# Attention scores with the query's two parts stacked on 128 partitions, in a two-layer hybrid encoder

## The chip, the core and the metric

The kernel runs on one core of a Trainium2 chip. The metric is device time in microseconds (us) of one execution, from the first to the last work on the core: 1370.9 us in the median of three runs before the change (1370.58 to 1371.35). A profile shows one further execution.

## What is computed

Two layers of an encoder over 512 tokens of 1024 channels, in float32. A layer normalizes x (an RMS norm with a scale and a shift made from a conditioning vector), projects it by `w_in` to 28 column blocks of 128, and hands these to three mixers: a gated depthwise convolution of width 31 over 256 channels, attention with 6 heads of 64, and a bidirectional gated recurrence (HGRN2) with 6 heads of 64. Their outputs together go through `w_out` into the residual. Then comes a gated MLP with a depthwise convolution of width 3. The attention is what matters here:

```python
scores = jnp.einsum('bnqhd,bnkhd->bhqk', qb, kb) * (Dh ** -0.5)   # Dh = 64
scores = scores - slopes[:, None, None] * dist
lse = jax.nn.logsumexp(scores, axis=-1)
p = jnp.exp(scores - lse[..., None])
...
wts = jax.nn.softmax(jnp.stack(lses, 0), axis=0)      # over three window/dilation pairs
att = jnp.einsum('gbsh,gbshd->bshd', wts, jnp.stack(outs, 0))
```

(The indices are cut.) The three windows with their mixture are one softmax over all 512 keys with a bias table a head, which is how the kernel computes it.

## The kernel before

**Layout.** Activations lie transposed, channels on the 128 partitions and the 512 tokens along the free dimension. TensorE multiplies in fp32r, so each operand of a large product is split into a high part, rounded to fp32r, and a low part, the rest: a product is three matmuls, high by high, high by low and low by high. The weights are split on the chip as they arrive (`wr` is the raw chunk, `wh` and `wl` its parts), the activations when they are made (`hx`).

**Engines.** Every TensorE matmul passes through the helper `mm` (L274), transposes through L280, and all work of VectorE (DVE) and ScalarE (ACT) through a wrapper (L181), so the profile's groups are told apart by tiles. SyncE (SP) issues all DMAs: weights, the tables for the conditioning (`wa`, `bias` from `w_ada`), and the attention's bias tables.

**Order.** The program is made of generators ("threads") that yield what they need next. A planner keeps a clock for each engine with a cost for each operation, and always lets run the thread of the best priority whose needs are met by that clock. What comes out is one fixed order of instructions on each engine. `span` tells the planner which stretch of a buffer an operand covers, and `written` when that stretch is ready. SBUF buffers come from small pools by tag (`BUFFERS`: size in KB a partition, count); what the MLP and the weight splitter keep is also taken from the pools of `MTAG`, `qk` among them.

**Mixers.** The projections run one column block after another (`REST`), 24 matmuls of 512 columns each into one of two PSUM banks `g`. `evac` takes a block out of PSUM. For the attention, a block of q or k holds a pair of heads, head 0 on partitions 0 to 63 and head 1 on 64 to 127. `evac` makes the high part with one ScalarE instruction (for k with whichever of ScalarE and VectorE the planner finds sooner) and the low part with one VectorE instruction, into one `qk` tile of two planes. There are three pairs a layer.

**Attention.** When q, k and v of a pair are out, `att` loads the two bias tables and starts eight `att_tile`, first the four query blocks of head 0 and then those of head 1, at most three under way. A tile is 128 queries by 512 keys:

```python
r = slice(64 * hd, 64 * hd + 64)
mm(sp, q[r, 0, s], k[r, 0], True, False)
mm(sp, q[r, 0, s], k[r, 1], False, False)
mm(sp, q[r, 1, s], k[r, 0], False, True)
```

These use 64 rows of the array, the upper or the lower half by the head. After it VectorE adds the bias and takes the minimum (q is negated, so the scores are too), ScalarE takes the exponential with its sum, the reciprocal and scaling follow on VectorE or ScalarE, then four transposes into PSUM and two copies into `PT`. When all eight are done, eight matmuls with v make the pair's output. The recurrence has small score matmuls of its own (64 by 32 blocks, `km`, `KK`, `QQ`).

Of the kernel before, what the change touches and what calls it, by code (L numbers as in the profile page):

```python
# [9 lines left out]
F32 = mybir.dt.float32  # L10
F32R = mybir.dt.float32r
# [8 lines left out]
T = 512  # L20
# [21 lines left out]
BUFFERS = dict(wr=(4, 3), wh=(4, 4), wl=(4, 4), hx=(4, 8), qk=(4, 2), PT=(4, 4), KK=(4, 1), QQ=(4, 1), S=(4, 1),  # L42
# [26 lines left out]
def span(ap):  # L69
    lo = hi = ap.offset  # L70
    for s, n in ap.ap[1:]:
        if s > 0:
            hi += s * (n - 1)
        else:
            lo += s * (n - 1)
    return lo, hi
# [116 lines left out]
class Kernel:  # L193
# [68 lines left out]
    def dma(self, out, in_, eng=None):  # L262
        (eng or self.nc.sync).dma_start(out=out, in_=in_)
        c = self.clk
        sb = out if in_.tensor.name in self.a_names else in_
        t = max(c.t.get("DMA", 0.0), c.t["PE"], c.written(sb) or 0.0, c.avail.get(sb.tensor.name, 0.0)) + size(sb) * sb.shape[0] * 4 / 350e3
        c.t["DMA"] = t
        if sb is out:
            lo, hi = span(out)
            c.w.setdefault(out.tensor.name, []).append((lo, hi, t + (4.5 if eng is self.nc.gpsimd else 2.4), "DMA"))  # L270
        c.last[sb.tensor.name] = t + 2.0

# [617 lines left out]
    def evac(self, l, n, ps):  # L890
# [51 lines left out]
        elif n >= Q_ATT:  # L942
            q = n < K_ATT
            p = n - Q_ATT if q else n - K_ATT
            yield (ps, "qk")
            t = self.sb([128, 2, T], "qk", F32R)
            if q:
                sc.activation(t[:, 0], ps, AF.Copy, scale=-0.125)
                yield (t[:, 0], DM)
                v.scalar_tensor_tensor(t[:, 1], ps, -0.125, t[:, 0].bitcast(F32), ALU.mult, ALU.subtract)  # L950
            else:
                self.copy(t[:, 0], ps)
                yield (t[:, 0], DM)
                v.tensor_tensor(out=t[:, 1], in0=ps, in1=t[:, 0].bitcast(F32), op=ALU.subtract)
            self.give(ps)
            cur["qa" if q else "ka", p] = t
# [243 lines left out]
    def att(self, l, p):  # L1200
# [8 lines left out]
        for hd in range(2):  # L1209
            for qt in range(4):  # L1210
                yield tuple(ths[-3:-2])
                ths.append(self.spawn(self.att_tile(q, k, bias[hd], PT[2 * hd:2 * hd + 2], hd, qt), AP, SLACK))
        yield tuple(ths) + (cur.pop(("Va", p)),)
        self.give(q, k, *bias)
# [18 lines left out]
    def att_tile(self, q, k, b, PT, hd, qt):  # L1233
        v, mm = self.v, self.mm
        r = slice(64 * hd, 64 * hd + 64)
# [3 lines left out]
        mm(sp, q[r, 0, s], k[r, 0], True, False)  # L1239
        mm(sp, q[r, 0, s], k[r, 1], False, False)  # L1240
        mm(sp, q[r, 1, s], k[r, 0], False, True)
# [195 lines left out]
```

## Time and profile before

| | |
|---|---|
| median of three runs | 1370.9 us |
| the profiled execution | 1370.76 us |
| its span, first to last instruction | 1369.0 us |
| mean granted TensorE clock | 0.991 |
| busy share of the span: PE, DVE, ACT | 98%, 78%, 45% |
| DMA | 169.19 MB, mean 124 GB/s |
| layer 0's mixers, layer 1's mixers | about 68 to 316 us, about 740 to 970 us |

The profiled execution is longer than its span by 1.8 us. In the profile PE is TensorE's matmul and PEld its weight load, a separate instruction that can run ahead of the matmuls. Matmuls overlap in their last part, so a single matmul's duration is longer than the distance to the next; costs are read from distances between starts. In a group's row stand engine, operation, output and inputs by tile name, shape, count, then busy time, the mean in ns of one, and the idle time before with what ended it. "issue" is time for which the profile shows nothing that was waited for.

### The profile page before, as it was taken

Reading aid. Unit: us, or ns where it says so; the run is one execution under the profiler, and the core shown is the slowest. Engines: PE = TensorE matmul, PEld = TensorE weight load, DVE = VectorE, ACT = ScalarE, POOL = GpSimd, SP = SyncE. Lnnn points to the kernel's source line nnn. Section 1 sums busy time; section 2 is a strip of 40 time slices with the busy share of each in tenths; the row PEclk is TensorE's granted clock in tenths of the full one; section 3 lists DMA queues with packets and bytes.
Section 4 is the critical chain, followed back from the end, with each engine's and each line's share of the span. In section 5 each row is a group of like instructions: output and inputs, shape, how many; then the busy total and the mean of one; then the engine's idle time right before and its main releaser. Section 6 shows DMA issues by size and latency. Waiting matters only on the chain.

```text
span 1369.0 us, 24502 instructions
## 1 busy us (share of the span) xinstructions
PE 1344.9 (98%) x10042; PEld 1112.4 (81%) x10042; DVE 1070.0 (78%) x1841; ACT 609.6 (45%) x1017; POOL 2.1 (0%) x16
## 2 busy tenths in 40 slices
PE   8999999999999999999999999999999999999997
PEld 7977767778988888888899777777898888888887
DVE  6799999898599999766695999888868565556666
ACT  4537556565342433333453473746535232233332
POOL 0000000000000000000000000000000000000000
PEclk8999999999999999999999999999999999999998
DMA  9534443232348788432431312011422323323221
GB/s 353 189 134 142 124 151 94 81 105 89 103 148 293 254 280 290 126 108 70 140 99 63 106 54 99 32 53 54 139 78 57 128 76 95 101 86 122 77 93 63
DMA packets 55264, 169.19 MB, mean 124 GB/s; under 512 B 6256, under 2 KB 8304, under 8 KB 55152
## 3 DMA queue, kind: packets, MB, share of 16 engines
q1 hardware_dynamic: 55152, 167.63, 37.9%
q8 instruction: 79, 1.29, 0.4%
q14 instruction: 33, 0.27, 0.1%
HBM read 165.50 MB, written 2.10 MB: 122 GB/s over the span
## 4 chain that ended last, share of the span: by engine, by line
PE 84%; DVE 12%; ACT 2%; issue 1%; DMA 0%; SPq 0%; DVEq 0%; ACTq 0%
PE m L274 53%; PE g L274 29%; DVE acc L181 2%; PE m L280 2%; DVE KK L181 2%; DVE QQ L181 1%; DVE wl L181 1%; DVE TT L181 1%; DVE wa L181 1%; DVE P L181 1%; DVE hx L181 1%; DVE x L181 1%; DVE st L181 0%; DVE sc L181 0%; DMA x<-xT 0%
## 5 line engine op out<-in xcount | busy, mean ns | idle before, releaser
L274 PE MATMUL g<-hx,wh 128*128 128x512 f32 (+1 forms) x1288 | 402.6, 390 | 0.9 <-DVE qk L181 0.8
L274 PE MATMUL m<-hx,wh 128*128 128x512 f32 (+1 forms) x1136 | 318.0, 364 | 0.0
L181 DVE TENSOR_TENSOR wl<-wr,wh 128x1024 fp32r<-128x1024 f32 (+3 forms) x215 | 220.5, 1027 | 90.4 <-ACT wh L181 79.4
L274 PEld LDWEIGHTS g<-hx,wh 128*128 128x128 f32 x1288 | 237.2, 189 | 53.2 <-issue 7.7
L181 ACT CAST wh<-wr 128x1024 fp32r<-128x1024 f32 (+3 forms) x176 | 157.1, 893 | 250.9 <-PE m L274 155.0
L274 PE MATMUL g<-hx,wl 128*128 128x512 f32 (+1 forms) x648 | 252.7, 390 | 0.0
L274 PEld LDWEIGHTS m<-hx,wh 128*128 128x128 f32 x1136 | 204.3, 189 | 34.2 <-issue 0.6
L274 PE MATMUL m<-hx,wl 128*128 128x512 f32 (+1 forms) x576 | 209.0, 363 | 0.0
L274 PEld LDWEIGHTS g<-hx,wl 128*128 128x128 f32 x648 | 122.5, 189 | 25.4 <-issue 3.8
L274 PEld LDWEIGHTS m<-hx,wl 128*128 128x128 f32 x576 | 108.7, 189 | 16.9
L181 DVE SCALAR_TENSOR_TENSOR x<-m,mod,x 128x256 f32<-128x256 f32 (+1 forms) x112 | 66.2, 592 | 43.1 <-PE m L274 42.1
L181 DVE SCALAR_TENSOR_TENSOR acc<-ap,par,acc 128x512 f32<-128x512 f32 x120 | 89.8, 748 | 2.2
L181 DVE SCALAR_TENSOR_TENSOR tmp<-m,par,tmp 128x511 f32<-128x511 f32 x120 | 89.1, 746 | 1.9
L181 ACT ACTIVATE P<-P,sm 128x512 f32<-128x512 f32 x72 | 51.5, 721 | 42.6 <-DVE sm L181 42.2
L181 ACT ACT_TABLE_LOAD x49 | 62.9, 1283 | 6.0 <-DVE sm L181 4.5
L181 DVE CAST wh<-wr 128x1024 fp32r<-128x1024 f32 (+3 forms) x41 | 24.5, 598 | 52.4 <-PE m L274 37.1
L181 ACT ACTIVATE tmp<-tmp 128x512 f32<-128x512 f32 x44 | 27.8, 632 | 73.1 <-DVE tmp L181 73.0
L181 ACT COPY km<-KK 128x512 f32<-128x512 f32 x30 | 20.5, 683 | 80.2 <-DVE KK L181 58.8
L181 ACT ACTIVATE tmp<-m,par 128x512 f32<-128x512 f32 x60 | 40.7, 686 | 34.5 <-PE m L274 32.8
L181 DVE CUSTOM_DVE_ANT_0 bias<-bias,cb,par 128x1024 f32<-128x1024 f32 x39 | 49.5, 1278 | 2.3 <-DMA bias<-w_ada 2.3
L181 DVE CUSTOM_DVE_ANT_0 wa<-wa,cb,par 128x1024 f32<-128x1024 f32 x39 | 49.9, 1278 | 0.7 <-DMA wa<-w_ada 0.7
L181 ACT ACTIVATE tmp<-x 128x256 f32<-128x256 f32 (+1 forms) x64 | 28.4, 444 | 46.4 <-DVE x L181 42.4
(319 smaller groups left out, 2158.0 us busy)
## 6 DMA issues: line engine op xcount, KB each, us to landing
wr<-w_up SPq DMA_DIRECT2D x76, 512.0 KB, 3.5
wr<-w_in SPq DMA_DIRECT2D x44, 512.0 KB, 3.5
bias<-w_ada SPq DMA_DIRECT2D x39, 512.0 KB, 4.5
wa<-w_ada SPq DMA_DIRECT2D x39, 512.0 KB, 4.0
wr<-w_down SPq DMA_DIRECT2D x32, 320.0 KB, 2.9
wr<-w_down SPq DMA_DIRECT2D x32, 256.0 KB, 2.6
wr<-w_in SPq DMA_DIRECT2D x16, 384.0 KB, 4.4
wr<-w_up SPq DMA_DIRECT2D x16, 384.0 KB, 3.3
```

The costliest lines, as they stand in the source:

```text
L181: r = f(*a, **k)
L274: self.nc.tensor.matmul(out, lhsT=lhsT, rhs=rhs, start=start, stop=stop, **kw)
L280: self.nc.tensor.transpose(out, in_, self.ident)
```

## The change

The query's high and low part of a head are put on top of each other: for head 0 the high part stays on partitions 0 to 63 and the low part is written to 64 to 127, for head 1 the other way round. The key gets a tile for each head, with the high part in plane 0 and the low part in plane 1; both are made on the head's own 64 partitions and then copied by one DMA (`shift`) to the other 64. A score tile is then two matmuls over all 128 partitions: (q high + q low) by k high, and the same by k low. The product of the two low parts, which was left out before, is now included.

So `evac` makes the parts a head at a time, on 64 partitions: two instructions where there was one, on ScalarE and on VectorE, for q and for k, and for k two DMAs on SP's queue. The `qk` pool has three buffers instead of two. `span` no longer counts the partition into the offset, so that the planner takes writes to different partition halves of a buffer as writes to the same stretch. The scratch space for dynamic DMA in SBUF is made smaller, which makes room for the buffer.

```diff
-BUFFERS = dict(wr=(4, 3), wh=(4, 4), wl=(4, 4), hx=(4, 8), qk=(4, 2), PT=(4, 4), ...
+BUFFERS = dict(wr=(4, 3), wh=(4, 4), wl=(4, 4), hx=(4, 8), qk=(4, 3), PT=(4, 4), ...
...
 def span(ap):
-    lo = hi = ap.offset
+    lo = hi = ap.offset % ap.ap[0][0]
...
+    def shift(self, out, in_):
+        self.nc.sync.dma_start(out=out.bitcast(F32), in_=in_.bitcast(F32))
+        c = self.clk
+        t = max(c.t.get("DMA", 0.0), c.t["PE"], c.written(in_) or 0.0) + size(in_) * in_.shape[0] * 4 / 350e3
+        c.t["DMA"] = t
+        lo, hi = span(out)
+        c.w.setdefault(out.tensor.name, []).append((lo, hi, t + 2.4, "DMA"))
+        c.last[out.tensor.name] = t + 2.4
...
-            yield (ps, "qk")
-            t = self.sb([128, 2, T], "qk", F32R)
+            own = [slice(0, 64), slice(64, 128)]
             if q:
-                sc.activation(t[:, 0], ps, AF.Copy, scale=-0.125)
-                yield (t[:, 0], DM)
-                v.scalar_tensor_tensor(t[:, 1], ps, -0.125, t[:, 0].bitcast(F32), ALU.mult, ALU.subtract)
+                yield (ps, "qk")
+                t = self.sb([128, 2, T], "qk", F32R)
+                for hd in range(2):
+                    sc.activation(t[own[hd], hd], ps[own[hd]], AF.Copy, scale=-0.125)
+                for hd in range(2):
+                    yield (t[:, hd], DM)
+                    v.scalar_tensor_tensor(t[own[1 - hd], hd], ps[own[hd]], -0.125, t[own[hd], hd].bitcast(F32),
+                                           ALU.mult, ALU.subtract)
             else:
-                self.copy(t[:, 0], ps)
-                yield (t[:, 0], DM)
-                v.tensor_tensor(out=t[:, 1], in0=ps, in1=t[:, 0].bitcast(F32), op=ALU.subtract)
+                yield (ps, ["qk", 2])
+                t = [self.sb([128, 2, T], "qk", F32R) for _ in range(2)]
+                for hd in range(2):
+                    self.copy(t[hd][own[hd], 0], ps[own[hd]])
+                for hd in range(2):
+                    yield (t[hd][:, 0], DM)
+                    v.tensor_tensor(out=t[hd][own[hd], 1], in0=ps[own[hd]], in1=t[hd][own[hd], 0].bitcast(F32),
+                                    op=ALU.subtract)
             self.give(ps)
+            if not q:
+                for hd in range(2):
+                    yield (t[hd],)
+                    self.shift(t[hd][own[1 - hd]], t[hd][own[hd]])
...
-        r = slice(64 * hd, 64 * hd + 64)
         s = slice(qt * 128, qt * 128 + 128)
         yield (q, k, "m")
         sp = self.pst("m")
-        mm(sp, q[r, 0, s], k[r, 0], True, False)
-        mm(sp, q[r, 0, s], k[r, 1], False, False)
-        mm(sp, q[r, 1, s], k[r, 0], False, True)
+        for i in range(2):
+            mm(sp, q[:, hd, s], k[:, i], i == 0, i == 1)
...
-    nc = bacc.Bacc("TRN2", target_bir_lowering=False, num_devices=1)
+    nc = bacc.Bacc("TRN2", target_bir_lowering=False, num_devices=1, dynamic_dma_scratch_size=1024)
```

The planner runs anew on all of this, so the order shifts throughout. Three places follow, in each the kernel before and then the changed one. A name is a buffer's tag with running numbers, so a number differs between the two kernels for the same thing; the lines are shifted by 10 (L274 is now L284).

On TensorE, the third pair of layer 0, from the last projection (V) to the first scores (`m_...<-qk,qk`):

```order
L274 MATMUL g_444_3067<-hx_18_198,wh_407_2791 128x512 x2
L274 MATMUL m_0_451_3103<-QQ_420_2874,km_442_3063 32x32 x32
L274 MATMUL g_444_3067<-hx_18_198,wl_412_2808 128x512
L274 MATMUL m_462_3159<-qk_445_3069,qk_426_2889 128x512 x3
L274 MATMUL m_463_3163<-qk_445_3069,qk_426_2889 128x512 x3
L280 MATMUL m_464_3167<-ident,tmp_453_3141 128x128 x4
```

```order
L284 MATMUL g_441_3031<-hx_18_199,wh_402_2732 128x512 x2
L284 MATMUL g_441_3031<-hx_18_199,wl_409_2761 128x512
L284 MATMUL g_460_3140<-hx_444_3046,wh_413_2798 128x512 x2
L284 MATMUL g_460_3140<-hx_444_3046,wl_416_2806 128x512
L284 MATMUL m_0_461_3144<-QQ_420_2841,km_451_3113 32x32 x32
L284 MATMUL m_463_3179<-qk_438_3021,qk_430_2909 128x512 x2
L290 MATMUL m_464_3182<-ident,tmp_453_3129 128x128 x4
```

The scores have moved behind the first three matmuls of the output projection (`g_460`), and they are two instead of three. Between the last matmul for k and the first score stand 24 full matmuls before and 27 now, with a group for the conditioning (`wa,cT`) and one more of the recurrence; for the second pair of the layer it is 27 and 32, with the same two and four transposes.

On VectorE, the first pair of layer 0, the low parts of q (`g_155`) and k (`g_163`) between steps of the recurrence (`KK`, `QQ`), the convolution (`acc`) and a weight's low part (`wl`):

```order
L181 SCALAR_TENSOR_TENSOR qk_162_1203<-g_155_1129,qk_162_1203 128x512
L181 SCALAR_TENSOR_TENSOR acc_120_866<-ap_137_935,par,acc_120_866 128x512
L181 TENSOR_TENSOR wl_172_1317<-wr_153_1125,wh_169_1278 128x1024
L181 TENSOR_TENSOR qk_170_1281<-g_163_1205,qk_170_1281 128x512
L181 TENSOR_TENSOR KK_122_869<-KK_122_869,TT_123_870 128x16x2x16
```

```order
L181 SCALAR_TENSOR_TENSOR qk_162_1204<-g_155_1130,qk_162_1204 64x512 x2
L181 TENSOR_TENSOR wl_173_1321<-wr_153_1126,wh_169_1280 128x1024
L181 TENSOR_TENSOR qk_170_1283<-g_163_1207,qk_170_1283 64x512
L181 TENSOR_TENSOR KK_123_872<-KK_123_872,TT_124_873 128x16x2x16
L181 TENSOR_TENSOR QQ_132_917<-QQ_132_917,TT_124_873 128x16x2x16
L181 COPY_PREDICATED sc_135_923<-msk,m_0_172_1288 128x256
L181 COPY S_134_922<-sc_135_923 32x8x32
L181 TENSOR_TENSOR TT_124_873<-TT_124_873 128x48
L181 TENSOR_TENSOR qk_171_1284<-g_163_1207,qk_171_1284 64x512
```

Each low part is two instructions now, and the second half of k comes after a step of the recurrence.

On SP, the DMAs of the second pair of layer 0 (`bias<-bias` are the two bias tables, `wa` and `wr` conditioning and weights):

```order
L263 DMA wr_306_2182<-w_in 128x1024
L263 DMA wa_307_2189<-w_sh 128x1024
L263 DMA bias_310_2198<-bias 128x896
L263 DMA bias_311_2199<-bias 128x896
L263 DMA wr_323_2262<-w_in 128x1024
```

```order
L263 DMA wr_308_2169<-w_in 128x1024
L263 DMA wa_309_2177<-w_sh 128x1024
L275 DMA qk_302_2112<-qk_302_2112 64x1024
L275 DMA qk_303_2113<-qk_303_2113 64x1024
L263 DMA bias_315_2240<-bias 128x896
L263 DMA bias_316_2241<-bias 128x896
L263 DMA wa_326_2278<-w_ada 128x1024
L263 DMA wr_328_2313<-w_in 128x1024
```

The two copies of k's parts stand ahead of the bias tables and of the next weights. Over the whole program VectorE has 12 more copies into `PT`, 10 fewer scalings of `P` and 4 more of the gates (`KK`, `TT`), which went from or to ScalarE.

More of the change, by code (lines that the diff above doesn't have):

```diff
@@ L39 @@
 H2 = T // 2
-BUFFERS = dict(wr=(4, 3), wh=(4, 4), wl=(4, 4), hx=(4, 8), qk=(4, 2), PT=(4, 4), KK=(4, 1), QQ=(4, 1), S=(4, 1),
+BUFFERS = dict(wr=(4, 3), wh=(4, 4), wl=(4, 4), hx=(4, 8), qk=(4, 3), PT=(4, 4), KK=(4, 1), QQ=(4, 1), S=(4, 1),
                TT=(6, 1), ao=(2, 2), vr=(2, 2), va=(2, 1), bias=(4, 2), wa=(4, 1), tmp=(2, 5), P=(2, 2), sc=(1, 1),
@@ L1211, in att @@
                 yield tuple(ths[-3:-2])
-                ths.append(self.spawn(self.att_tile(q, k, bias[hd], PT[2 * hd:2 * hd + 2], hd, qt), AP, SLACK))
+                ths.append(self.spawn(self.att_tile(q, k[hd], bias[hd], PT[2 * hd:2 * hd + 2], hd, qt), AP, SLACK))
         yield tuple(ths) + (cur.pop(("Va", p)),)
-        self.give(q, k, *bias)
+        self.give(q, *k, *bias)
         V = cur["va"]
```

## The prediction

> **What bounds the kernel now.** I read the page's engine totals and its chain first, then windows cut by stage, then the chain in order of time, and last the PE timeline around one score tile.
>
> ```profile
> PE 1344.9 (98%) x10042; PEld 1112.4 (81%) x10042; DVE 1070.0 (78%) x1841; ACT 609.6 (45%) x1017; POOL 2.1 (0%) x16
> PE 84%; DVE 12%; ACT 2%; issue 1%; DMA 0%; SPq 0%; DVEq 0%; ACTq 0%
> ```
>
> TensorE fills the span, and VectorE has the rest of the chain. The windows (span, then busy us of PE, PEld, DVE, ACT, POOL, the clock, DMA share, GB/s) say where: 68 to 316 is layer 0's mixers, 740 to 970 layer 1's, 450 to 500 a piece of an MLP.
>
> ```profile
> 68.00:316.00 248.00, 241.09 (x2639) 177.24 (x2637) 226.14 (x434) 143.40 (x256) 0.00 (x0) 0.99 0.38 118
> 740.00:970.00 230.00, 228.54 (x2544) 172.54 (x2543) 206.44 (x397) 133.63 (x239) 0.00 (x0) 1.00 0.22 71
> 100.00:120.00 20.00, 20.00 (x233) 15.65 (x233) 19.57 (x40) 11.22 (x22) 0.00 (x0) 1.00 0.56 177
> 750.00:780.00 30.00, 30.00 (x494) 23.35 (x492) 29.71 (x46) 11.30 (x19) 0.00 (x0) 1.00 0.29 92
> 180.00:250.00 70.00, 69.73 (x716) 51.47 (x716) 63.29 (x128) 43.32 (x83) 0.00 (x0) 0.98 0.40 128
> 450.00:500.00 50.00, 50.00 (x223) 41.39 (x222) 48.63 (x77) 19.07 (x28) 0.00 (x0) 1.00 0.76 245
> ```
>
> In the MLP TensorE runs without a gap, and there are no scores. In the mixers VectorE is busy 91.2% (226.1 of 248) and 89.8% (206.4 of 230), and 97.9% and 99.0% in the dense pieces: two engines share the bound there. The chain (start, length) runs over full matmuls in one place and over VectorE's steps in another:
>
> ```profile
> 380.04 10.88 PE g L274 x48
> 842.04 0.60 DVE qk L181
> 842.64 0.59 DVE KK L181
> ```
>
> So a full 512-column matmul costs 10.88/48 = 0.227 us, and a VectorE instruction of 512 columns holds the next one back 0.60.
>
> **What it removes.** Three 64-row matmuls a tile become two of 128 rows. The timeline (start, us, ...) and the weight load behind it, one tile between projections; then the first and last of the score stretches, and the one odd one; then their group:
>
> ```profile
> 137.27 0.40 PE L274 MATMUL g<-hx,wh 128*128 128x512 f32 x1
> 137.60 0.96 PE L274 MATMUL m<-qk,qk 64*128 64x512 f32 x3
> 138.49 0.50 PE L274 MATMUL g<-hx,wh 128*128 128x512 f32 x1
> 138.83 0.40 PE L274 MATMUL g<-hx,wl 128*128 128x512 f32 x1
> 138.49 0.19 PEld L274 LDWEIGHTS g<-hx,wh 128*128 128x128 f32 x1 [0.37 <-issue]
> 106.54 2.35 PE L274 MATMUL m<-qk,qk 64*128 64x512 f32 x9
> 954.56 0.96 PE L274 MATMUL m<-qk,qk 64*128 64x512 f32 x3
> 793.18 0.97 PE L274 MATMUL m<-qk,qk 64*128 64x512 f32 x6
> L274 PE MATMUL m<-qk,qk 64*128 64x512 f32 x144 | 43.2, 420 | 1.0 <-DVE qk L181 0.3 <-DVE sm L181 0.3 <-ACT tmp L181 0.2
> ```
>
> A matmul less for each of 48 tiles is 48 x 0.227 = 10.9 us. The larger part is the change of height: 137.27 to 138.83 is 1.56 us for five matmuls, and five at 0.227 are 1.14, so going to 64 rows and back costs 0.42; the weight load at 138.49 starts late, with its matmul, instead of running ahead. Nine scores in a row pay it once. The PE timeline has 38 such stretches from 106.54 to 954.56, 21 in layer 0 and 17 in layer 1. At full height they pay nothing: layer 0 saves 21 x 0.42 + 24 x 0.227 = 14.3 us, layer 1 17 x 0.42 + 5.4 = 12.6. At 793.18 two heads' tiles already run side by side (six matmuls in the time of three); that is lost, 0.7. TensorE's sum is 26.2 us, nearest possible time 1370.8 - 26.2 = 1344.6.
>
> **What it adds.**
>
> ```profile
> L181 DVE SCALAR_TENSOR_TENSOR qk<-g,qk 128x512 fp32r<-128x512 f32 x6 | 4.1, 684 | 0.0
> L181 ACT COPY S<-m 32x256 f32<-32x256 f32 x24 | 8.7, 361 | 0.2
> L181 ACT COPY PT<-m 128x256 f32<-128x256 f32 x60 | 19.0, 373 | 2.2 <-PE m L280 2.2
> L181 DVE COPY PT<-m 128x256 f32<-128x256 f32 x36 | 13.5, 416 | 5.6 <-ACT PT L181 5.6
> L181 DVE TENSOR_SCALAR P<-P,sm 128x512 f32<-128x512 f32 x24 | 11.7, 487 | 0.8
> L181 DVE TENSOR_SCALAR KK<-KK,lb 128x512 f32<-128x512 f32 x6 | 2.9, 479 | 0.0
> L274 PE MATMUL g<-hx,wh 128*128 128x512 f32 (+1 forms) x1288 | 402.6, 390 | 0.9 <-DVE qk L181 0.8
> ```
>
> The low parts are now made in halves of 64 partitions. A 32-partition copy of 256 columns takes 361 ns and a 128-partition one 373, so fewer partitions are no cheaper on ScalarE, and I take the same for VectorE: 12 more instructions at 0.60, 3.6 us a layer (were a half worth half, 0). The high parts do the same on ScalarE, some 0.59 each; it is busy 143 of 248, and this hides there (if not, 0.6 a pair, 3.5 in all). The last row is the third cost: the two PSUM banks of the projections are freed only when the low parts are made, and TensorE already waits 0.8 us for that; with one more VectorE instruction ahead of each release it can wait up to 12 x 0.60 = 7.2 us. That is a wait of TensorE on VectorE, and I count it inside the density below, not beside it. The planner also deals other work anew; by the order VectorE gets 12 more copies into PT (5.0), 10 fewer scalings of P (-4.9) and 4 more of the gates (1.9): 1.0 a layer. So VectorE holds 226.1 + 4.6 = 230.7 us in layer 0 and 211.0 in layer 1.
>
> That decides the gain. With VectorE no denser than today (about 90.5%) the mixers would grow, 230.7/0.912 = 253 and 211/0.898 = 235, 10 us more. As dense as its best pieces (98.5%) it would leave TensorE's 26.2 whole. The stretches where TensorE leads now (180 to 250, VectorE at 90%) have both some room and waits of their own, so I take the middle, 94.5%: 244.1 and 223.3, or 3.9 + 6.7 = 10.6 us gained.
>
> **The shift.** Twelve DMAs copy k's parts to the other half.
>
> ```profile
> wr<-w_out SPq DMA_DIRECT2D x16, 256.0 KB, 2.6
> x<-xT SPq DMA_DIRECT2D x8, 256.0 KB, 5.7
> bias<-bias SPq DMA_DIRECT2D x12, 448.0 KB, 5.3
> 100.32 0.33 SPq L263 DMA_DIRECT2D wr<-w_in  x1
> 100.21 0.68 DVE L181 TENSOR_TENSOR qk<-g,qk 128x512 fp32r<-128x512 f32 x1
> 180.27 0.69 DVE L181 TENSOR_TENSOR qk<-g,qk 128x512 fp32r<-128x512 f32 x1
> 181.92 0.96 PE L274 MATMUL m<-qk,qk 64*128 64x512 f32 x3
> 262.26 0.69 DVE L181 TENSOR_TENSOR qk<-g,qk 128x512 fp32r<-128x512 f32 x1
> 263.01 1.43 PE L274 MATMUL m<-qk,qk 64*128 64x512 f32 x5 [0.34 <-DVE qk L181]
> 775.46 0.68 DVE L181 TENSOR_TENSOR qk<-g,qk 128x512 fp32r<-128x512 f32 x1
> 777.92 0.96 PE L274 MATMUL m<-qk,qk 64*128 64x512 f32 x3
> 183.45 0.67 PE L274 MATMUL m<-wa,cT 128*32 128x128 f32 x16
> 746.32 0.69 PE m L274 x47
> ```
>
> No transfer from SBUF to SBUF stands in the trace; the nearest of 256 KB land in 2.6 us (queue calm) to 5.7 (start). I take 2.6, as these queues are calm. With 0.33 of issue and a VectorE step of 0.60, k is ready 3.5 us later than today. On SP the shift waits for VectorE; behind it stand the two bias loads, which the first softmax instruction needs, and weight loads. Layer 0's second pair has 1.0 us to spare today (180.96 to 181.92), and the order now puts five full matmuls and two small groups ahead of its scores, 1.1 + 0.67 + 0.69: covered. The third pair waits 0.34 today; ahead of it now stand three matmuls and the same two groups, 2.0: it stalls 3.5 + 0.3 - 2.0, about 1.7. Layer 0's first pair has 5.6 us (100.89 to 106.54), which covers it. Layer 1's first has 1.8 (776.14 to 777.92), and four more matmuls and a further group of small scores come ahead of it, 0.9 + 0.69, with six transposes: just covered; its other two pairs have over 4 us. So 1.7 in all. Bounds 0 and 8: at a landing of 5.7 three pairs stall some 3 us more each than their cover, less what VectorE's lag hides of it. The bias loads leave behind the second shift, 0.66 of issue and a VectorE step later than today, and land after 5.3: with 0.33 of their own that is some 6.3 us behind k's first low part. The order keeps at least ten VectorE instructions, 6 us at 0.60, between the last low part and the first softmax, so I cost that at nothing; if the cover is short, VectorE itself stands still, by up to 1.3 us a pair.
>
> The third qk buffer and the planner's changed view of partition halves move the order elsewhere too: in the MLP TensorE stands at 50.00 of 50.00 and cannot gain; I take 0, within 2 either way. **Sum**: 1370.76 (span 1369.0, 1.8 around it; the median is 1370.9) - 10.6 + 1.7 = 1361.9, said as **1362**.
>
> **Rivals.**
> A, *TensorE stays the bound*: VectorE packs denser as it stops waiting for TensorE, and 17 to 26 us come out, 1344.6 to 1354. For it: 97.9 and 99.0% do occur. Against: only in short pieces. 0.14.
> B, *VectorE takes it all*: the break-even densities are 230.7/248 = 93.0% and 211/230 = 91.7%; there the time stays at 1368.2 to 1373.6. 0.12.
> C, *slower by VectorE*: 12 halves and the moved work lengthen an engine that paces both tails, and its density stays below those marks; 1374 to 1381, the last at today's. It decides once the densities in the two windows come out under 93.0 and 91.7. Against: the scores stand in stretches led by TensorE as well. 0.12.
> D, *side by side was worth more*: were all tiles of two heads paired as at 793.18, they would fill 72 matmul times, 16.3 us, and the change's 96 fill 21.8: 5.5 slower, 1376. But one stretch of 38 is so, since a head's tiles follow one another; 0.02. [...]
>
> **Numbers.** The forecast, some of TensorE's gain with VectorE as second bound, 1354 to 1368, has 0.60. 0.2%, or 2.7 us, is about what a measurement tells from no change. Faster is forecast and A, 0.74; same B, 0.12; slower C and D, 0.14. The range 1350 to 1375 cuts half of A and most of C.
>
> **What would show it.** The scores' group at 128 rows, x96, with full matmuls 0.227 apart on both sides; VectorE's busy share in the mixers up to some 94%; a qk DMA landing near 2.6 us, and a wait of TensorE for it only in layer 0's third pair. It is wrong if the share stays near 90%, if TensorE waits for qk at several pairs, or if TensorE's waits for VectorE do not grow at all.

## The result, and the profile after

The changed kernel takes 1394.7 us in the median of four runs (1393.9 to 1396.4), the kernel before beside it 1370.8 (1370.6 to 1371.4): a ratio of 1.0175, 95% interval 1.0158 to 1.0193. It is 23.9 us slower. The forecast was 1362, range 1350 to 1375, faster.

The totals and the chain of the changed kernel's page:

```profile
span 1392.4 us, 24478 instructions
PE 1338.1 (96%) x9994; PEld 1115.3 (80%) x9994; DVE 1082.6 (78%) x1858; ACT 620.6 (45%) x1026; POOL 2.1 (0%) x16
PE 77%; DVE 16%; ACT 4%; issue 2%; DMA 1%; SPq 0%; DVEq 0%; ACTq 0%
```

TensorE works 6.8 us less than before, but the part of the span in which it is not busy grew from 24.1 us (1369.0 - 1344.9) to 54.3. The rows that the change was made for came out as predicted. Here is one score tile on the PE timeline (start, length), the scores' group by shape, the low parts' groups, and the transfer with its landing:

```profile
976.32 0.39 PE L284 MATMUL g<-hx,wl 128*128 128x512 f32 x1
976.55 0.62 PE L284 MATMUL m<-qk,qk 128*128 128x512 f32 x2
977.01 0.39 PE L284 MATMUL g<-hx,wh 128*128 128x512 f32 x1
977.24 0.49 PE L290 MATMUL m<-ident,P 128*128 128x128 f32 x3
L284 PE MATMUL m<-qk,qk x96: 387/396/628, 106.7 to 976.8; 128*128 128x512 f32 x96
L181 DVE SCALAR_TENSOR_TENSOR qk<-g,qk 64x512 fp32r<-64x512 f32 x12 | 8.3, 689 | 0.3
L181 DVE TENSOR_TENSOR qk<-g,qk 64x512 fp32r<-64x512 f32 x12 | 8.3, 688 | 0.2
qk<-qk SPq DMA_DIRECT2D x12, 256.0 KB, 4.0
```

Four matmuls from 976.32 to 977.24 are 0.23 each: nothing is paid for the height any more, and this tile with its neighbours takes 0.92 us for the 1.56 of before. Half as many partitions cost VectorE the same (689 ns; 684 before on 128).

Now the mixers, VectorE's and TensorE's busy time in each (from the first convolution tap to the last mixer output, rounded to 1 us; first the kernel before, then the change):

```profile
74.00:317.00 243.00, 235.48 (x2614) 172.47 (x2612) 221.46 (x427) 141.86 (x254) 0.00 (x0) 0.99 0.38 120
747.00:971.00 224.00, 222.54 (x2455) 167.75 (x2455) 200.86 (x387) 130.23 (x232) 0.00 (x0) 1.00 0.23 74
```

```profile
74.00:325.00 251.00, 226.67 (x2583) 169.86 (x2581) 228.82 (x439) 142.55 (x252) 0.00 (x0) 0.96 0.38 122
758.00:995.00 237.00, 221.54 (x2439) 169.96 (x2437) 207.33 (x397) 137.37 (x239) 0.00 (x0) 0.96 0.25 77
```

Layer 0's mixers grew by 8 us and layer 1's by 13, which is nearly all of the loss. VectorE's work grew by 7.4 and 6.5 us, and its share did not rise: 91.1% to 91.2%, and 89.7% to 87.5%. The granted clock of TensorE (third from the end of each row) fell from 0.99 to 0.96 and from 1.00 to 0.96. By an estimate from these rows that is worth at most some 10 us of matmul time in each layer's mixers, against 2 and 0 before; at most, as it counts idle time too.

A mixer can be cut along its three recurrences, by starts on the timelines: from the first small score matmul of a recurrence to its first output matmul ("recurrence"), from there to the next one's first score ("between"), and from the third recurrence's first output matmul to the last mixer output ("tail").

| us | recurrences | between | tail |
|---|---|---|---|
| layer 0 before | 50.5 + 50.1 + 54.3 = 154.9 | 36.3 + 32.9 = 69.2 | 18.0 |
| layer 0 after | 48.9 + 53.0 + 47.7 = 149.6 | 35.9 + 26.6 = 62.5 | 38.3 |
| layer 1 before | 43.2 + 43.4 + 37.7 = 124.3 | 42.8 + 31.3 = 74.1 | 26.3 |
| layer 1 after | 45.3 + 47.4 + 55.2 = 147.9 | 41.8 + 25.5 = 67.3 | 22.8 |

Between the recurrences, where TensorE makes the next one's projections, 6.7 and 6.8 us were gained. They are lost in layer 0's tail (+20.3) and in layer 1's recurrences (+23.6, of which 17.5 in the third). The end of the convolution stands in both places. The convolution's taps are VectorE's filler work, taken when nothing of better priority is ready; behind the last tap stands a serial piece: means on TensorE, square root on ScalarE, a long reciprocal on VectorE, gating, split. In layer 0 the last tap starts at 240.44 before (first row) and, by the timeline of the change, at about 305.1, the last of the three that start at 303.50; then come VectorE's and TensorE's rows of its tail:

```profile
240.44 0.74 DVE L181 SCALAR_TENSOR_TENSOR acc<-ap,par,acc 128x512 f32<-128x512 f32 x1
```

```profile
303.50 2.32 DVE L181 SCALAR_TENSOR_TENSOR acc<-ap,par,acc 128x512 f32<-128x512 f32 x3
313.44 3.35 DVE L181 RECIPROCAL t<-t 128x512 f32<-128x512 f32 x1 [3.70 <-ACT t L181]
305.87 1.12 PE L284 MATMUL m<-acc,onesC 128*128 128x512 f32 x2 [1.30 <-DVE acc L181]
309.25 3.43 PE L284 MATMUL m<-tmp,onesC 128*128 128x512 f32 x4 [2.26 <-ACT tmp L181]
320.19 1.31 PE L284 MATMUL m<-hx,wa 128*128 128x256 f32 x2 [7.51 <-ACT hx L181]
324.19 1.31 PE L284 MATMUL m<-hx,wh 128*128 128x256 f32 x2 [2.48 <-ACT hx L181]
```

The four waits in brackets are 13.6 us in which TensorE stands still; before, its waits for these outputs were 0.80 and 0.34 by its timeline. In layer 1 the last tap starts at 904.6 (883.2 before), and the tail falls into the third recurrence, which begins at 917.0:

```profile
920.73 3.35 DVE L181 RECIPROCAL t<-t 128x512 f32<-128x512 f32 x1 [2.88 <-ACT t L181]
925.22 0.69 ACT L181 COPY km<-KK 128x512 f32<-128x512 f32 x1 [4.26 <-DVE KK L181]
```

VectorE waits 2.88 us for the square root and then divides for 3.35, with the recurrence's step queued behind; ScalarE's next copy for the recurrence waits 4.26 for it. Before, that reciprocal ran at 893.74, ahead of the third recurrence (907.0).

This accounts for a part of the 17.5 us only. In the kernel before, the same reciprocal lay inside layer 0's third recurrence (first row), and that one took 54.3 us against 47.7 in the change: by an estimate from these two, some 7 us. VectorE also has some 10 us more of work in layer 1's third recurrence, at a lower clock of TensorE (before, then the change):

```profile
255.47 3.35 DVE L181 RECIPROCAL t<-t 128x512 f32<-128x512 f32 x1 [3.18 <-ACT t L181]
907.00:945.00 38.00, 36.74 (x653) 27.82 (x652) 33.56 (x73) 20.33 (x40) 0.00 (x0) 1.00 0.23 68
917.00:972.00 55.00, 49.99 (x707) 39.40 (x705) 43.40 (x87) 31.66 (x56) 0.00 (x0) 0.94 0.19 57
```

### The profile page after: what moved, and what is told of

The parts are those of the page before. It is cut to its first block, busy times and chain, and to the rows that moved or that the text cites. A ratio compares the mean times of both kernels' runs of the same rounds, so it can differ in the third digit from the quotient of the medians.

```text
span 1392.4 us, 24478 instructions
## 1 busy us (share of the span) xinstructions
PE 1338.1 (96%) x9994; PEld 1115.3 (80%) x9994; DVE 1082.6 (78%) x1858; ACT 620.6 (45%) x1026; POOL 2.1 (0%) x16
## 4 chain that ended last, share of the span: by engine, by line
PE 77%; DVE 16%; ACT 4%; issue 2%; DMA 1%; SPq 0%; DVEq 0%; ACTq 0%
PE m L284 50%; PE g L284 26%; DVE acc L181 3%; DVE wl L181 2%; DVE QQ L181 2%; DVE KK L181 2%; PE m L290 1%; DVE qk L181 1%; DVE TT L181 1%; DVE wa L181 1%; DVE P L181 1%; DVE st L181 1%; ACT P L181 1%; DVE x L181 1%; ACT wh L181 1%
## 5 line engine op out<-in xcount | busy, mean ns | idle before, releaser
L284 PE MATMUL g<-hx,wh 128*128 128x512 f32 (+1 forms) x1288 | 407.0, 392 | 3.4 <-DVE qk L181 2.7
L284 PE MATMUL m<-hx,wh 128*128 128x512 f32 (+1 forms) x1168 | 325.5, 363 | 3.0 <-ACT hx L181 2.5
L181 DVE TENSOR_TENSOR wl<-wr,wh 128x1024 fp32r<-128x1024 f32 (+3 forms) x211 | 216.0, 1025 | 81.8 <-ACT wh L181 76.6
L284 PEld LDWEIGHTS g<-hx,wh 128*128 128x128 f32 x1288 | 238.3, 190 | 50.2 <-DVE qk L181 3.5
L284 PE MATMUL g<-hx,wl 128*128 128x512 f32 (+1 forms) x644 | 251.0, 390 | 0.0
L284 PEld LDWEIGHTS m<-hx,wh 128*128 128x128 f32 x1168 | 210.0, 189 | 37.7 <-ACT hx L181 2.8
L284 PE MATMUL m<-hx,wl 128*128 128x512 f32 (+1 forms) x568 | 207.0, 364 | 0.0
L284 PEld LDWEIGHTS g<-hx,wl 128*128 128x128 f32 x644 | 122.4, 190 | 23.3 <-issue 0.8
L284 PEld LDWEIGHTS m<-hx,wl 128*128 128x128 f32 x568 | 107.4, 189 | 16.9
L181 ACT ACTIVATE P<-P,sm 128x512 f32<-128x512 f32 x82 | 58.3, 722 | 57.3 <-DVE sm L181 57.0
L181 DVE CAST wh<-wr 128x1024 fp32r<-128x1024 f32 (+3 forms) x38 | 23.0, 605 | 50.5 <-PE m L284 37.1
```

The source lines that it names most:

```text
L181: r = f(*a, **k)
L284: self.nc.tensor.matmul(out, lhsT=lhsT, rhs=rhs, start=start, stop=stop, **kw)
```

## The experiments

Three theories stood at the start. A: VectorE bounds the mixers; what TensorE saves is time in which VectorE did the convolution. B: the planner's corrected view alone spoils the order. C: the split evacuations and the transfers are the loss. Later runs set O (the order as such) and others beside them, as their expectations say. The kernel before stayed at 1370.2 to 1371.2 beside all of them; differences below are against 1370.8.

**The planner's view alone.**

```diff
 (kernel before)
-    lo = hi = ap.offset
+    lo = hi = ap.offset % ap.ap[0][0]
```

> The kernel before with one edit of the change alone: the planner's view of which part of a tile an access covers (the modulo in span); scores, evacuations, buffers and transfers stay. Theory A (VectorE bounds the mixers; what TensorE saves is taken from the time in which VectorE did the convolution, whose tail then stands exposed): the view adds no work, so 1367 to 1374 us. Theory B (the corrected view alone reorders the mixers badly): 1385 to 1395 us, most of the 24 us. Theory C (the doubled low-part evacuations and the transfers are the loss): 1367 to 1374 us.

1379.8 us, ratio 1.0061 (1.0046 to 1.0076). A line that asks for no work of its own costs 9 us, over a third of the loss. It lies between the theories: above the 1367 to 1374 of A and C, below the 1385 to 1395 of B.

**The full-height matmuls alone.**

```diff
 (kernel before)
-        mm(sp, q[r, 0, s], k[r, 0], True, False)
-        mm(sp, q[r, 0, s], k[r, 1], False, False)
-        mm(sp, q[r, 1, s], k[r, 0], False, True)
+        for i in range(2):
+            mm(sp, q[:, 0, s], k[:, i], i == 0, i == 1)
```

> The kernel before with TensorE's part of the change alone: two full-height matmuls a tile on the old query and key tiles (the scores then mix both heads, so this part of the computation is changed); evacuations, view, buffers as before, no transfers. TensorE's saving by the prediction is 26.2 us. Theory A: VectorE has the same work in less time, so at most half of it arrives: 1357 to 1372 us, the convolution's last tap of layer 0 later than the 240.4 us of before. Theories B and C: the saving arrives nearly whole, 1344 to 1350 us.

1368.2 us, ratio 0.9981 (0.9971 to 0.9990). Its page:

```profile
PE 1329.1 (97%) x9994; PEld 1111.4 (81%) x9994; DVE 1071.1 (78%) x1846; ACT 618.0 (45%) x1017; POOL 2.1 (0%) x16
```

TensorE works 15.8 us less (1344.9 before), the time falls by 2.6. That lies in theory A's range. With the old constants the saving is worth next to nothing even without split evacuations and transfers.

**The changed kernel with its scores undone.**

```diff
 (changed kernel; query's low part kept on its own half)
-        for i in range(2):
-            mm(sp, q[:, hd, s], k[:, i], i == 0, i == 1)
+        mm(sp, q[r, 0, s], k[r, 0], True, False)
+        mm(sp, q[r, 0, s], k[r, 1], False, False)
+        mm(sp, q[r, 1, s], k[r, 0], False, True)
```

> The changed kernel with three 64-row score matmuls a tile again (query's low part written to its own half; as many evacuation instructions and the same transfers as in the change, whose copies on the other half are then not read). TensorE has its 26 us of work back. Theory A: VectorE's work is unchanged and sets the time, so 1385 to 1402 us, within 8 us of the change. Theories B and C: the work comes on top, 1410 to 1421 us.

1390.3 us, ratio 1.0139 (1.0124 to 1.0154), as theory A had it.

```profile
PE 1350.6 (97%) x10042; PEld 1114.7 (80%) x10042; DVE 1082.1 (78%) x1861; ACT 622.3 (45%) x1023; POOL 2.1 (0%) x16
```

With 12.5 us more TensorE work than the change (1338.1) it is 4.4 us faster.

**The changed kernel with the old view.**

```diff
 (changed kernel)
-    lo = hi = ap.offset % ap.ap[0][0]
+    lo = hi = ap.offset % ap.ap[0][0] if ap.tensor.name.startswith("qk") else ap.offset
```

> The changed kernel with the planner's old view for all tiles but the query's and key's. Theory A: as the change, 1388 to 1397 us. Theory B: the loss of the view goes, 1362 to 1375 us. Theory C: 1388 to 1397 us.

1383.7 us, ratio 1.0083 (1.0067 to 1.0100): 11 us faster than the change, between the theories. The view costs about as much in both kernels. The mixers of the two layers:

```profile
75.00:315.00 240.00, 224.83 (x2585) 169.68 (x2584) 227.11 (x437) 144.19 (x254) 0.00 (x0) 0.98 0.41 128
747.00:983.00 236.00, 220.74 (x2503) 171.05 (x2483) 208.02 (x399) 139.30 (x240) 0.00 (x0) 0.97 0.26 79
```

VectorE's share of layer 0 is 94.6% here, and these mixers are 3 us shorter than in the kernel before (243). Layer 1's share is 88.1%, and its mixers are 12 us longer (224 before).

**The split evacuations alone**, on top of the new view.

```diff
 (kernel before with the new view; the query alike)
-                self.copy(t[:, 0], ps)
 ...
-                v.tensor_tensor(out=t[:, 1], in0=ps, in1=t[:, 0].bitcast(F32), op=ALU.subtract)
+            for o in own:
+                self.copy(t[o, 0], ps[o])
+            for o in own:
 ...
+                v.tensor_tensor(out=t[o, 1], in0=ps[o], in1=t[o, 0].bitcast(F32), op=ALU.subtract)
```

> The kernel before with the new view (1379.8 us by itself) and the query's and key's evacuations done in halves of 64 partitions, as many instructions as in the change, but to the old places: no transfers, three 64-row score matmuls. What the twelve extra low-part halves and twelve extra high-part halves a layer cost by themselves. Theory A (VectorE's time is what the mixers lack): 7 us more VectorE work in all, 1384 to 1391 us. Theory C (the transfers and the wait for them made the 10.6 us between the view alone, 1379.8, and the change with its scores undone, 1390.3): 1378 to 1382 us.

1403.5 us, ratio 1.0240 (1.0225 to 1.0255): 24 us over the view alone, far above both theories, and 13 above the undone change, which has the same evacuations and, besides, the transfers and the third buffer. (The extra low parts are six a layer, not the twelve that the expectation names; its 7 us in all is reckoned with six.)

```profile
PE 1357.4 (97%) x10042; PEld 1118.2 (80%) x10042; DVE 1080.1 (77%) x1852; ACT 629.0 (45%) x1034; POOL 2.1 (0%) x16
```

VectorE has 8.4 us more to do than with the view alone (1071.7 there), the time grows by 24. So the prices of these edits do not add up, and are no property of the edits alone: with each the planner lays out another order.

**A short convolution**, which takes 45 us off VectorE, in the kernel before, with the full-height matmuls alone, and in the change.

```diff
-        for i in range(1, CW):
+        for i in range(1, 11):
```

> The kernel before with 11 of the convolution's 31 taps (the convolution is cut short): 40 tap instructions of 0.66 us, 26 us of VectorE time, less in each mixer. TensorE is busy in 97% of layer 0's mixer already, so the time falls little: 1355 to 1370 us by all theories. The reference for the next two.

> The full-height matmuls alone (on the old tiles, so the scores mix both heads) and 11 of the 31 taps. Theory A: with VectorE relieved, TensorE's saving of 26 us now arrives for the greater part: 14 to 26 us under the short-convolution kernel before, where with all taps it was 2.6 us. If the saving were never there in TensorE's time, or the order of the work swallows it whatever VectorE has to do: 0 to 6 us under it.

> The changed kernel with 11 of the 31 taps. Theory A: the doubled evacuations no longer cost their time either; what is left is TensorE's 26 us less and the view's 9 us more at most: 5 to 22 us under the short-convolution kernel before. If the transfers or the order make the loss: 5 to 24 us above it.

1377.3 us for the kernel before (1371.5 to 1380.8), 1361.6 with the full-height matmuls, 1384.1 for the change; their ratios to the kernel before are 1.0040 (1.0022 to 1.0058), 0.9933 (0.9918 to 0.9948) and 1.0094 (1.0079 to 1.0109). The page of the first:

```profile
PE 1349.9 (98%) x10042; PEld 1115.3 (81%) x10042; DVE 1025.0 (74%) x1777; ACT 600.4 (44%) x998; POOL 2.1 (0%) x16
```

With 45 us less VectorE work (1070.0 before) the kernel is 6.5 us slower in the median, and above the expected 1355 to 1370 in every run. That ends theory A in its plain form, in which the amount of VectorE work sets the time. The second stands 15.8 us under the first, as theory A expected (14 to 26), where with all taps the same edit gave 2.6; 9.2 of it lies below the kernel with all taps. The change stands 6.7 above the first, not below it. What is left is theory O: an order laid out for one kernel and kept fixed; where pieces like the convolution's tail land in it decides. These three runs do not show it by themselves; the next two were made for it.

**Only the order, only the sharing.** In the change, the convolution ahead of recurrence and attention; apart from it, copies moved towards ScalarE.

```diff
 (changed kernel)
-CP = 2.5
+CP = 0.9
...
 (changed kernel, another run)
-BIAS = 0.8
+BIAS = 1.2
```

> The changed kernel with the convolution's taps ahead of recurrence and attention in the planner's priorities (CP 2.5 to 0.9; work unchanged). Theory O (order: the convolution is put last, so its serial tail stands exposed at the end of layer 0 and inside the third recurrence of layer 1): both go, 1370 to 1384 us, layer 0's stretch from the third recurrence's output to the last mixed output under 28 us (38.3 in the change, 18.0 before). Theory A (the amount of VectorE work, wherever it is put): what the convolution gains the recurrences lose, 1388 to 1400 us.

> The changed kernel with the rule that shares copies between ScalarE and VectorE moved by 0.4 us towards ScalarE (BIAS 0.8 to 1.2), which gives VectorE less and ScalarE more of the same copies. Theory A: 1378 to 1388 us. Theory O: as the order then falls, the convolution's place deciding; if its last tap in layer 0 comes before 270 us (305.1 in the change), 1375 to 1388, otherwise 1388 to 1400 us.

The first takes 1381.7 us, ratio 1.0079 (1.0064 to 1.0094), 13 less than the change with the same work (VectorE 1083.2 us, 1082.6 in the change). As theory O expected, layer 0's tail is 18.5 us (38.3 in the change), and layer 1's third recurrence 47.2 (55.2). But layer 0's third recurrence grew from 47.7 to 62.1, as theory A had it, and TensorE's longest wait in it is one of 6.40 us for the attention's `P`:

```profile
286.45 1.11 PE L290 MATMUL m<-ident,P 128*128 128x128 f32 x4 [6.40 <-ACT P L181]
```

By the same cut layer 0's mixers are only 4 us shorter than in the change (247 against 251) and layer 1's 16 (221 against 237), of which 11 between the recurrences. So this run shows that the order alone is worth 13 us; it does not show that the place of the convolution's tail is what they come from.

The second takes 1371.7, ratio 1.0007 (0.9997 to 1.0016): one constant gives back 23 of the 24 us, more than either theory had. Its page:

```profile
PE 1327.1 (97%) x9994; PEld 1108.7 (81%) x9994; DVE 1056.1 (77%) x1806; ACT 657.8 (48%) x1082; POOL 2.1 (0%) x16
```

VectorE has 26.5 us less to do than in the change (1082.6) and ScalarE 37.2 more; the last tap of layer 0 starts at 246.2 by the timeline, not 305.1. Whether the lighter VectorE or the new order did it, this run doesn't tell.

**An order of its own for each.** The planner's constants set anew for the change, and for the kernel before, so that the planner's own clock ends early. (The constants, one to a line in the code, are gathered here.)

```diff
 (changed kernel)
-SLACK, LAG, WAR, WA, SM = 0.5, 5, 0.1, 5, 0.2
-ADAI, EV, RP, DM, ADAP, ADAM, BIAS = 0.0, 0.5, 1.0, 1.0, 1.0, 2.0, 0.8
+SLACK, LAG, WAR, WA, SM = 0.3, 6, 0.0, 4, 0.1
+ADAI, EV, RP, DM, ADAP, ADAM, BIAS = 1.0, 1.5, 1.2, 1.6, 0.45, 3.0, 1.5
...
 (kernel before)
-SLACK, LAG, WAR, WA, WM = 0.5, 5, 0.1, 5, 4
-EV, RP, AP, DM, ADAP, BIAS = 0.5, 1.0, 2.0, 1.0, 1.0, 0.8
+SLACK, LAG, WAR, WA, WM = 0.2, 6, 0.0, 4, 2
+EV, RP, AP, DM, ADAP, BIAS = 1.5, 1.2, 0.7, 1.6, 2.7, 1.5
```

> The changed kernel with the planner's constants (priorities, slacks, due times, the sharing rule) set anew for it; the computation is the same. Theory O: the order was set for the old kernel and costs the change its gain, so a new one gives 1352 to 1368 us, faster than before. Theory A: VectorE's work is the same to a few us, so 1375 us or more.

> The kernel before with the same constants set anew for it, as the control of the run with the change's. Theory O: it was near its own best order, 1358 to 1370 us, and the change with its own order is 3 to 12 us faster than this. Theory A: 1358 to 1370 us, and the change with its own order is slower than this by 10 us or more.

1368.9 us for the change and 1369.0 for the kernel before, both ratios 0.9984 (0.9975 to 0.9993 and 0.9994). So 26 us of the change's time went with the constants, which lay out the order and share the copies (VectorE 1048.7 against 1082.6); theory A had ruled that out. But the gain that theory O promised is not there either. The pages, the change first:

```profile
span 1366.2 us, 24470 instructions
PE 1326.1 (97%) x9994; PEld 1108.1 (81%) x9994; DVE 1048.7 (77%) x1789; ACT 661.4 (48%) x1097; POOL 2.1 (0%) x16
```

```profile
span 1367.2 us, 24509 instructions
PE 1343.3 (98%) x10038; PEld 1111.6 (81%) x10038; DVE 1034.7 (76%) x1767; ACT 656.7 (48%) x1091; POOL 2.1 (0%) x16
```

TensorE works 17.2 us less, and the rest of the span is 16.2 us more (40.1 against 23.9). By the same cut as above the change gains 16.9 and 12.0 us between the recurrences of the two layers (59.1 against 76.0, 64.9 against 76.9), and loses 21.0 in layer 0's tail (37.1 against 16.1) and 12.8 in layer 1's recurrences (138.4 against 125.6). In that tail of the change, from 273.8 on, all taps are done (the last starts at 261.9), and TensorE's one long wait is for the attention's `P`:

```profile
302.61 1.11 PE L290 MATMUL m<-ident,P 128*128 128x128 f32 x4 [6.46 <-ACT P L181]
```

**What takes the gain when the order is good.** The full-height matmuls alone with constants of their own; the change and the kernel before with the short convolution and constants of their own.

```diff
 (full-height matmuls alone)
+SLACK, LAG, WAR, WA, WM, CM, CP = 0.2, 6, 0.0, 4, 2, 0.8, 1.5
+RP, AP, DM, ADAM, BIAS = 0.45, 1.1, 1.15, 1.0, 1.2
...
 (short convolution, each with its own constants)
+        for i in range(1, 11):
```

> The kernel before with the full-height score matmuls alone (old tiles, so both heads are mixed; no split evacuations, no transfers, old view) and planner constants set anew for it. Both earlier kernels with constants of their own took 1369. Theory E (the split evacuations and the transfers eat TensorE's 22 us when the order is good): 1346 to 1356 us. Theory V (something else than TensorE holds the mixers, VectorE's queue and the chains through it, so that less TensorE work alone only makes idle time): 1360 to 1369 us.

> The changed kernel with 11 of the convolution's 31 taps and planner constants set anew for that. To be held against the next one, the kernel before treated alike. If the amount of VectorE work is what holds the mixers, 10 to 22 us below the next; if the length of the chains (recurrence, attention) holds them whatever VectorE has to do, within 4 us of it.

> The kernel before with 11 of the 31 taps and planner constants set anew for that. TensorE is busy 97 to 99% of the mixers in the old kernel with its own constants (1369), so it can fall little: 1356 to 1368 us by either theory.

The full-height matmuls alone reach 1358.7 us, ratio 0.9908 (0.9892 to 0.9925), between the two theories: 10.3 under the kernel before with its own order. So about half of TensorE's saving can be had; in the whole change, with the order found for it, none is left. Each kernel was given one such order, though, and single constants moved the change by 13 and 23 us: that a difference of 10 us between two orders is the edit's own is not shown. With the short convolution the change takes 1354.8 and the kernel before 1364.6: 9.7 less, just short of what the amount of VectorE work was to give (10 to 22) and outside the other case (4). So with fewer taps the change does gain once each kernel has an order of its own. Whether the amount of VectorE work does it or the convolution's early end (last tap of layer 0 at 149.9, against 261.9 with all taps) is not told apart. What keeps the rest of TensorE's saving even then (17.7 us less busy, 9.7 less time) was not isolated.

The page of the matmuls alone with its own constants, and its layer 0 mixers:

```profile
PE 1324.3 (98%) x9990; PEld 1107.6 (82%) x9990; DVE 1043.2 (77%) x1790; ACT 644.2 (47%) x1068; POOL 2.1 (0%) x16
74.00:305.00 231.00, 220.31 (x2584) 167.82 (x2582) 215.39 (x416) 144.31 (x261) 0.00 (x0) 1.00 0.37 121
```

TensorE works 19.0 us less than in the kernel before with its own order. VectorE is at 93.2% of layer 0 (215.39 of 231); in the change and in the kernel before with their own orders its windows there give 91.5% and 91.0%.

**Taps on GpSimd.** Half the taps moved from VectorE to the idle engine, in the kernel before.

```diff
+        if n == 0:
 ...
+            for i in range(1, CW):
 ...
+                g.tensor_scalar(u, a[:, i:i + T], w(i), None, ALU.mult)
+                g.tensor_tensor(out=acc, in0=u, in1=acc, op=ALU.add)
```

> The kernel before with the taps of one of the convolution's two channel groups on GpSimd (a multiplication and an addition each), which is idle otherwise; constants as before. VectorE loses 31 taps of 0.66 us, 20 us a layer, and nothing is left out. If GpSimd's work does not disturb VectorE and the order falls no worse: 1362 to 1372 us; if the two share a path to memory and slow each other: above 1378 us, with VectorE's rows longer than in the kernel before.

1448.6 us, ratio 1.0557 (1.0540 to 1.0573), the second case. VectorE's groups of the remaining taps and of the attention's bias step, before and here:

```profile
L181 DVE SCALAR_TENSOR_TENSOR acc<-ap,par,acc 128x512 f32<-128x512 f32 x120 | 89.8, 748 | 2.2
L181 DVE CUSTOM_DVE_ANT_0 P<-m,bias 128x512 f32<-128x512 f32 x48 | 32.5, 684 | 5.5 <-PE m L280 4.9 <-issue 0.4
```

```profile
L181 DVE SCALAR_TENSOR_TENSOR acc<-ap,par,acc 128x512 f32<-128x512 f32 x60 | 63.4, 1057 | 1.1
L181 DVE CUSTOM_DVE_ANT_0 P<-m,bias 128x512 f32<-128x512 f32 x48 | 32.3, 684 | 6.1 <-PE m L280 3.9 <-ACT tmp L181 1.8
L181 POOL TENSOR_SCALAR t<-ap,par 128x512 f32<-128x512 f32 x60 | 126.5, 2108 | 5.7
```

A tap on VectorE, whose two operands lie in SBUF, goes from 748 to 1057 ns in the mean of this run; the bias step, which reads one operand from PSUM, stays at 684, though a third of its 48 run beside GpSimd by the timelines. So with work on GpSimd VectorE's taps took longer; that the two share a path to memory, as the expectation supposes, is not shown. The move costs 78 us; how much of it are the longer taps and how much the new order was not taken apart.

**The key evacuated once**, the fastest of the whole changes, and its control.

```diff
 (changed kernel, old view outside query and key, constants of its own)
-                for hd in range(2):
-                    self.copy(t[hd][own[hd], 0], ps[own[hd]])
-                for hd in range(2):
-                    v.tensor_tensor(out=t[hd][own[hd], 1], in0=ps[own[hd]], ...)
+                self.copy(t[0][:, 0], ps)
 ...
+                v.tensor_tensor(out=t[0][:, 1], in0=ps, in1=t[0][:, 0].bitcast(F32), op=ALU.subtract)
...
+                for o in own:
+                    self.shift(t[1][o], t[0][own[1]])
+                yield (t[1],)
+                self.shift(t[0][own[1]], t[0][own[0]])
```

> The change with the key's evacuation done once on 128 partitions (one copy and one low part a pair, as before) and three transfers a pair in place of two: the odd head's key to both halves of the second tile, then the even head's over the freed half of the first; the old view but for query and key, planner constants of its own; nothing left out. It takes three of the six extra low parts a layer off VectorE and three extra copies, and adds a second transfer behind the first. If the split evacuations hold back half of TensorE's saving (form alone with its own order: 1358.7; with them, 1368.9), 1356 to 1365 us, faster than both kernels. If the transfers hold it back, 1368 to 1378 us.

> The changed kernel as it is, but with the old view for all tiles except query and key and with planner constants of its own: the control of the run with the key evacuated once. As the retuned change with the new view (1368.9), less up to 8 for the view: 1361 to 1370 us.

1365.6 us, ratio 0.9957 (0.9941 to 0.9974), just above the first case (1356 to 1365), and 1367.7 for the control, ratio 0.9976 (0.9965 to 0.9986). With half as many transfers again, landing in 4.5 us, it is 2.1 us faster. That speaks for the key's split evacuation costing more than its transfers, but does not show it: the two intervals overlap a little, each has an order of its own, and the planner counts 4.0 us for a landing in the first and 2.4 in the control; the 7 us left to the 1358.7 of the matmuls alone (the query's split, the transfers, the view) were not taken apart.

## Why the prediction was wrong, point by point

**What it removes: right by the tile.** The 0.42 us for the change of height is gone, and the predicted 0.65 a tile was 0.64. In busy time, whose ends are modelled, 15.8 to 19.0 us show for the forecast 26.2 (1344.9 to 1329.1, 1343.3 to 1324.3); the 6.8 in the change itself fit its lower granted clock in the mixers (0.96). No kernel here turned more than 10.3 us of that into time with all 31 taps.

**The density: the step that failed.** "I take the middle, 94.5%", the term of -10.6 us; the mixers grew by 21. VectorE came to 91.2% and 87.5%, at or below its old share, and under both marks (93.0 and 91.7) from which rival C was to decide. The 97.9 and 99.0% behind that middle were rows of 20 and 30 us. Taken over a mixer the share holds the waits in VectorE's own queue as well, and a quicker TensorE alone did not take these away. Nor is the old share a ceiling: in the change with the old view layer 0 reached 94.6%, and its mixers gained 3 us where 3.9 were forecast, while layer 1 fell to 88.1% and lost 12. So the share came out of the order, and the prediction took it as a number to be chosen. Its own alternative, "no denser than today", gave 10 us more in the two layers together; 21 were measured.

**"the planner's changed view ... I take 0, within 2 either way": wrong.** By itself it costs 9.0 us, and its removal from the change gives 11. The price was never to be found in a row of durations, for the line asks for no work; it was in the order. The third buffer was not tried apart.

**The added VectorE work: too small.** Forecast 4.6 us a layer, found 7.4 and 6.5. The half-height instruction cost what was assumed, as much as a whole one (689 ns against 684).

**The shift: about right in size, wrong in place.** The landing is 4.0 us, not the 2.6 taken, and inside the bounds 2.6 to 5.7. TensorE waited once for it, 1.3 us by the timeline, in layer 1's first pair (796.52) and not in layer 0's third; 1.7 were forecast. That the sizes are near is in part luck, as the place differs.

```profile
796.52 0.73 PE L284 MATMUL m<-qk,qk 128*128 128x512 f32 x2 [1.34 <-DMA qk<-qk]
```

**The rivals.** C had the sign and the condition, but its mechanism was VectorE's amount spread evenly, 1381 at most. The other 14 us are of the size that one priority, with the same work, gave back (13), and can be the order's. That they come from the convolution's tail, late at the end of layer 0 and inside the last recurrence of layer 1, is read from the trace and not shown apart. C was given 0.12. A (TensorE stays the bound) never occurred. B's time, no change, is what the two kernels have with an order of their own, but through a balance of gain and loss that it did not foresee. Pairs side by side (D) were not tried.

Shown by runs: the saving on TensorE, the view's price, the price of the order (13 us by one priority; 26 by all constants, which share the copies too), and that with the orders found for them the whole change is worth nothing and the matmuls alone 10. Only argued: that the convolution's tail is the piece that decides, and that filler work was pushed back *because* the matmuls went faster. The undone change, with all its TensorE work, also has a late last tap in layer 0 (285.8 by its timeline), so the split evacuations and the view push as well.

## What to carry to other kernels

Where two engines are as busy in a stage as here (TensorE 97% and VectorE 91% of layer 0's mixers before), time taken off one can turn into waiting: the full-height matmuls alone took 15.8 us off TensorE's work and 2.6 off the time. Do not take a share between the second engine's mean and its best short pieces as what it will reach: over layer 0's mixers it came to 91.2% in the change and to 94.6% in the same change with the old view. Where a planner lays out a fixed order, ask first which filler work with a serial end runs in the holes that the change closes, and where that end will then stand. And compare two kernels each with an order of its own before judging an edit: here the whole change was worth +24 or 0 us, and the matmuls alone -2.6 or -10, by the order they were put in.

## What was not expected of the hardware

One pause of TensorE cost more than its length. After the 7.51 us wait above, matmuls of 256 columns ran at about half the speed that they had from 330.0 on, and the granted clock, third from the end of the last two rows, was 0.50 and then 1.00:

```profile
325.52 0.63 PE L284 MATMUL m<-hx,S 128*128 128x256 f32 x2
325.94 0.41 PE L284 MATMUL m<-hx,wl 128*128 128x256 f32 x1
330.42 0.40 PE L284 MATMUL m<-hx,S 128*128 128x256 f32 x2
330.65 0.28 PE L284 MATMUL m<-hx,wl 128*128 128x256 f32 x1
317.00:330.00 13.00, 7.04 (x28) 6.16 (x29) 8.16 (x14) 5.84 (x9) 0.00 (x0) 0.50 0.15 43
331.00:344.00 13.00, 13.00 (x109) 12.95 (x108) 9.27 (x19) 4.57 (x11) 0.00 (x0) 1.00 0.24 72
```

Two take 0.42 us from start to start at 325.52 and 0.23 at 330.42, so the 4.5 us up to 330.0 lost about 2, by an estimate from these distances. The trace has a pause of 7.51 us, then slow matmuls from 320.19, a second pause of 2.48 us, and slow ones again from 324.19 to about 330.0, 5.8 us. What sets the length of the slow stretch is not shown.

In the run with half the taps on GpSimd, VectorE's own taps, which have two operands in SBUF, took 41% longer in the mean (748 to 1057 ns), and the bias step, which reads PSUM, no longer than before (684). What makes the difference between the two is not shown.
